# GpSimd's ring of gathers written out for six turns, and eighteen waits behind its drain

## The chip, the cores and the metric

The kernel runs on one core of one Trainium2 chip. The metric is the device time of one execution in microseconds. A profile is one recorded execution; its span runs from the first to the last instruction of the program and is shorter than the device time.

## What is computed

```python
def reference(x, lengths, w):            # x: 8 x 8192 x 512 float32, w: 512 x 512
    mask = (pos < lengths[:, None, None])
    cs = np.cumsum(x * mask, axis=1)
    midpoints = (lengths // 2).clip(0)
    mid_features = cs[b_idx, midpoints, :]
    return np.matmul(mid_features[:, None, :], w).squeeze(1)
```

For each of the 8 sequences, the rows of x from the first to the one at half the sequence's length are added up, and the sum is multiplied by w. The lengths are data, so the program learns only when it runs how many rows it has to read.

## The kernel before, in words

**The sum as a matrix product.** Rows of x lie on 128 partitions, and TensorE multiplies them by a small matrix of zeros and ones with one column for each sequence. A row that doesn't belong to a sequence's first half gets a zero. The products are accumulated in the PSUM tiles `s_ps` and `d_ps`.

**Three sources of rows.** The first 256 rows of every sequence are read whatever the lengths are. Rows 64 to 255 are loaded by two transfers on SyncE's queue at the start, into two slots of the tile `xt`. Rows 0 to 63 go into `xb`, by two transfers that GpSimd issues at the end (line 257). All rows from 256 on are gathered in units of 8 rows, 128 units (2 MiB) at a time, by an indirect DMA that GpSimd issues (line 228, in `fetch`). With the given lengths there are 13 gathers. They go round the three slots of `xt` (`R = 3`).

**The engines' parts in the round.** TensorE waits for a slot's data, multiplies it (line 395) and counts `s_done` up. ScalarE waits for that count, copies the next column of unit numbers into `now` (line 185, `s_now`) and the next zeros and ones into `ww`. GpSimd waits for `s_now`, issues the gather into the slot that has come free, and takes `s_now` back (line 252). SyncE relays the landings to TensorE. Each engine's round is a ring of program blocks: the function `ring` writes out `R` turns; before each the engine compares a register with the turn's number (line 126) and leaves the ring when no turn is left; after the last one it lowers the register (line 130) and jumps back (line 131). The first three gathers stand ahead of GpSimd's ring (blocks `gp_b_0` to `gp_b_2`).

**The end.** Behind its ring GpSimd issues six transfers: two for `xb`, and four for w into `wt`: a half (line 259), a quarter (line 261) and the two halves of the last quarter (line 263; `s_w[3]` counts the last of them). Then it runs a drain (line 264), and waits for the two stores of the output (`s_out` at 32, line 265, carried by the branch of line 266). TensorE waits for `xb` (`s_back`), for the copies of the sums into SBUF by VectorE and ScalarE, and for each piece of w, and multiplies the sums by w into `o_ps`. VectorE and ScalarE copy that to `o_sb`; SyncE and ScalarE store one half each (line 207). The branch leads GpSimd to the program's end, where all engines meet and GpSimd clears the semaphores.

Of the kernel before, what the change touches and what calls it, by code (L numbers as in the profile page):

```python
# [15 lines left out]
def kernel(  # L16
# [22 lines left out]
    R = 3  # L39
# [6 lines left out]
    C = -(-B * (S // 2 // U + 1 - HU) // P)  # L46
    FAR = 1 << 17
    IDLE = 2
    xu = x.rearrange("b (q u) d -> (b q) (u d)", u=U)
    lens_words = lengths.tensor.reshape([B]).bitcast(I32).ap().rearrange("(o t) -> o t", o=1)  # L50

# [8 lines left out]
    def sem(name):  # L60
        return tc.alloc_semaphore(name)
# [45 lines left out]
    s_back = [sem(f"back{k}") for k in range(PARTS)]  # L107
    s_w = [sem(f"w{k}") for k in range(4)]
# [11 lines left out]
    def weights_by_rows(at, n):  # L120
        return ww[:, at * B:(at + n) * B].rearrange("p (u b) -> p u b", b=B)

    def ring(eng, name, left, body):
        for s in range(R):
            with nc.body(f"{name}_0_{s}", valid_engines=[eng.engine]):
                eng.br_cmp(left, s, f"{name}_1_{s}", f"{name}_end", "IS_GT")  # L126
            with nc.body(f"{name}_1_{s}", valid_engines=[eng.engine]):
                body(s)
                if s == R - 1:
                    eng.reg_sub(left, left, R)  # L130
                eng.br(f"{name}_0_{(s + 1) % R}")


    def sync(sp):
        left = sp.alloc_register("left_sp")
        full = sp.alloc_register("full_sp")
        have = sp.alloc_register("have_sp")
        sp.reg_mov(full, 16)
        sp.reg_mov(have, 1)
        sp.wait_ge(s_dve, marks["count"])  # L140
        sp.load(left, count[:])
        sp.wait_ge(s_dve, marks["front"])
        sp.wait_ge(s_zero, 3)
        for f in range(PARTS):
            sp.wait_ge(s_front[f], 16)
            sp.sem_inc(s_rdy, 1)
        sp.br("sy_0_0")

        def relay(s):
            sp.wait_ge(s_wr, have)  # L150
            sp.wait_ge(s_full[s], full)
            sp.sem_inc(s_rdy, 1)
            sp.reg_add(have, have, 1)
            if s == R - 1:
                sp.reg_add(full, full, 16)

        ring(sp, "sy", left, relay)
        with nc.body("sy_end", valid_engines=[sp.engine]):
            sp.wait_ge(s_dve, marks["out0"])
            sp.wait_ge(s_act, 3)  # L160
            store(sp, 0)
            sp.br(END)


    def scalar(act):
# [16 lines left out]
        def weigh(s):  # L182
# [7 lines left out]
            act.reg_add(turn, turn, 1)  # L190

        ring(act, "ac", left, weigh)
        with nc.body("ac_end", valid_engines=[act.engine]):
            act.wait_ge(s_pe, 2)
# [15 lines left out]
    def gpsimd(pool):  # L210
        pool.iota(v_i[:], pattern=[[P * U, C], [1, U]], base=HEAD, channel_multiplier=0)
        pool.iota(r_i[:, FU:], pattern=[[2, BU], [-(BU // 2), FB]], base=0,
                  channel_multiplier=BU // 2).then_inc(s_pool, 1)
        pool.wait_ge(s_pool, 1)
        for k in range(4):
            pool.iota(at_i[32 * k:32 * k + 32], pattern=[[P, C]],
                      base=64 * (k % 2) + 8 * (k // 2) + 63 * 8 * k,
                      channel_multiplier=16).then_inc(s_pool, 1)
        pool.tensor_scalar(out=row[:, 2 * B + 2:], in0=lens[:, ::2], scalar1=0.5, scalar2=0.25,
                           op0=ALU.mult, op1=ALU.add)._wait_ge(s_len, 16).then_inc(s_pool, 1)  # L220
        pool.wait_ge(s_pool, 6)
        pool.iota(r_i[:, :FU], pattern=[[2, FU], [-(FU // 2), FB]], base=2 * TOP,
                  channel_multiplier=FU // 2)
        pool.iota(fold_i[:], pattern=[[-32, 2], [-1, B]], base=P, channel_multiplier=1,
                  ).then_inc(s_pool, 1)

        def fetch(to, units, at, n, full):
            return pool.indirect_dma_start(  # L228
                out=to, out_offset=None, in_=units,
                in_offset=bass.IndirectOffsetOnAxis(ap=at, axis=0),  # L230
                bounds_check=n - 1, oob_is_err=False).then_inc(full, 16)

        left = pool.alloc_register("left_pool")
        pool.wait_ge(s_dve, marks["idx"])
        pool.br("gp_b_0")
        for c in range(R):
            if c > 0:
                with nc.body(f"gp_a_{c}", valid_engines=[pool.engine]):
                    pool.br_cmp(left, c, f"gp_b_{c}", "gp_end", "IS_GT")
            with nc.body(f"gp_b_{c}", valid_engines=[pool.engine]):  # L240
                got = fetch(xt[:, c], xu, now[:, c:c + 1], B * UB, s_full[c])
                if c > 0:
                    got._wait_ge(s_done, c)
                if c == 0:
                    pool.load(left, count[:])  # L245
                if c == R - 1:
                    pool.reg_sub(left, left, R)
                pool.br(f"gp_a_{c + 1}" if c + 1 < R else "gp_0_0")

        def gather(s):  # L250
            fetch(xt[:, s], xu, now[:, s:s + 1], B * UB, s_full[s])._wait_ge(s_now, 1)
            pool.sem_inc(s_now, -1)  # L252

        ring(pool, "gp", left, gather)
        with nc.body("gp_end", valid_engines=[pool.engine]):
            for f in range(PARTS):
                pool.dma_start(out=xb[:, f], in_=x[FB * f:FB * (f + 1), :TOP].rearrange(  # L257
                    "b (q u) d -> q b (u d)", u=BU)).then_inc(s_back[f], 16)
            pool.dma_start(out=wt[:, :2], in_=w[HALVES[0]].rearrange("(p k) d -> p k d", k=2),
                           ).then_inc(s_w[0], 16)  # L260
            pool.dma_start(out=wt[:, 2], in_=w[QUARTERS[2]]).then_inc(s_w[1], 16)
            for g, at in enumerate(HALVES):
                pool.dma_start(out=wt[:, 3, at], in_=w[QUARTERS[3], at]).then_inc(s_w[2 + g], 16)  # L263
            pool.drain()
            pool.wait_ge(s_out, 32)
            pool.br(END)

# [125 lines left out]
    def tensor(pe):  # L393
# [5 lines left out]
        def idle(n):  # L399
            for _ in range(n):  # L400
                pe.matmul(idle_ps[:FB], lhsT=ones[:, :FB], rhs=ones[:, :1].to_broadcast((P, D)),  # L401
                          start=True, stop=True, skip_group_check=True)
# [24 lines left out]
        with nc.body("pe_idle", valid_engines=[pe.engine]):  # L427
            idle(IDLE)
            pe.br("pe_to")
# [4 lines left out]
        with nc.body("pe_end", valid_engines=[pe.engine]):  # L434
# [17 lines left out]
            for k in range(KC):  # L452
# [10 lines left out]

    programs = [(nc.vector, vector, "dv"), (nc.sync, sync, "sy"), (nc.scalar, scalar, "ac"),
                (nc.gpsimd, gpsimd, "gp")]
    for f in range(PARTS):
        nc.sync.dma_start(out=xt[:, f + 1, :FU * D], in_=x[FB * f:FB * (f + 1), TOP:HEAD].rearrange(
            "b (q u) d -> q b (u d)", u=FU)).then_inc(s_front[f], 16)
    nc.scalar.dma_start(out=lens[:], in_=lens_words).then_inc(s_len, 16)
    left = nc.tensor.alloc_register("left_pe")  # L470
# [37 lines left out]
```

## Time and profile before

| what | value |
|---|---|
| device time, median of 3 (lowest, highest) | 83.02 us (82.86, 83.16) |
| span of the profiled execution | 80.4 us |
| busy: TensorE, VectorE, ScalarE, GpSimd | 59.6, 11.8, 9.7, 19.9 us |
| bytes read from HBM over the span | 32.51 MB |
| a gather's issue on GpSimd, from issue to landing | 0.98 us, 11.7 us |
| start of one gather to the start of the next in the ring | 4.9 us |

In a group's row the page gives line, engine, operation, tiles and shape, the number of instructions, then the busy time, the mean of one in nanoseconds, and the idle time ahead of them with what ended it. Engine names: PE is TensorE, PEld its weight loads, DVE is VectorE, ACT ScalarE, POOL GpSimd, SP SyncE; a small q behind a name (POOLq) marks what the engine's sequencer does alone, such as branches, semaphore and register steps. They are not counted as busy. The busy TensorE is in part idle work: 58 of its multiplications write `idle_ps`, which nothing reads.

### The profile page before, as it was taken

What the parts mean: (1) busy time and instruction counts of PE and PEld (TensorE: products, weight loads), DVE (VectorE), ACT (ScalarE), POOL (GpSimd) and SP (SyncE); (2) the same over time, 40 slices, a digit from 0 to 9 for tenths busy, and PEclk for the clock granted to TensorE, in tenths of its full rate; (3) what the DMA queues carried; (4) which work ended last, traced back from release to release, by engine and by line L of the source; (5) the groups of instructions that cost most, each with busy time, mean ns of one, the idle gap of its engine ahead of it and who ended that gap; (6) DMA issues with size and microseconds to landing.
All of it is one profiled execution on the core that took longest, in us unless ns stands there. A gap on an engine that the chain in (4) does not pass through costs nothing.

```text
span 80.4 us, 1176 instructions
## 1 busy us (share of the span) xinstructions
PE 59.6 (74%) x360; PEld 14.1 (18%) x360; DVE 11.8 (15%) x43; ACT 9.7 (12%) x31; POOL 19.9 (25%) x32
## 2 busy tenths in 40 slices
PE   0599998997693957939488493975939679399940
PEld 0212212120110202112020110201102021112820
DVE  0799300891000000000000000000000000003130
ACT  2971010102010010201001020010100100000220
POOL 5432050754022040310404004040220793000000
PEclk9999999999999999999999999999999999999998
DMA  0899999999999999999999999999999999999700
GB/s 0 299 428 434 442 418 432 432 424 448 399 456 416 432 432 432 440 399 448 432 415 448 432 424 416 432 448 399 448 432 424 416 432 448 399 373 409 285 0 8
DMA packets 2803, 31.23 MB, mean 388 GB/s; under 512 B 434, under 2 KB 450, under 8 KB 962
## 3 DMA queue, kind: packets, MB, share of 16 engines
q0 software_dynamic: 2480, 28.05, 82.4%
q1 hardware_dynamic: 304, 3.15, 9.7%
q8 instruction: 1, 0.02, 0.1%
q10 hardware_dynamic: 18, 0.01, 0.0%
HBM read 32.51 MB, written 0.02 MB: 404 GB/s over the span
## 4 chain that ended last, share of the span: by engine, by line
issue 59%; POOL 14%; DMA 14%; PE 5%; DVE 2%; POOLq 2%; ACTq 0%; SPq 0%
POOL xt L228 14%; DMA xb<-in_x_dram 12%; DMA lens<-in_lengths_dram 1%; PE mf_ps L446 1%; PE o_ps L395 1%; PE d_ps L395 1%; PE bc_ps L408 1%; DVE o_sb L276 1%; POOL xb L257 1%; POOLq L245 1%; PE mf_ps L449 1%; POOLq L228 0%; DVE row L276 0%; POOLq L126 0%; DVE ge L276 0%
## 5 line engine op out<-in xcount | busy, mean ns | idle before, releaser
L395 PE MATMUL s_ps<-xt,ww 128*8 128x512 f32 x240 | 29.5, 598 | 14.6 <-PEq L415 14.6
L401 PE MATMUL idle_ps<-ones 128*4 128x512 f32 x58 | 29.6, 637 | 0.0
L228 POOL DMA_INDIRECT xt<-in_x_dram,now x13 | 14.8, 1135 | 45.9 <-POOLq L252 36.7
L395 PEld LDWEIGHTS s_ps<-xt,ww 128*8 128x8 f32 x240 | 5.9, 89 | 37.8 <-issue 37.6
L276 DVE COPY s_sb<-s_ps 128x256 f32<-128x256 f32 x2 | 0.8, 420 | 55.3 <-PE s_ps L395 55.3
L401 PEld LDWEIGHTS idle_ps<-ones 128*4 128x4 f32 x58 | 5.1, 90 | 20.4 <-issue 20.4
L185 ACT COPY now<-idx 128x1 int32 x10 | 1.9, 192 | 44.1 <-PE s_ps L395 44.1
L276 DVE TENSOR_TENSOR early<-v_f,ends 128x192 f32<-128x192 f32 (+1 forms) x2 | 2.4, 1192 | 5.5 <-PE s_ps L395 5.5
L408 PE MATMUL bc_ps<-row,ones 1*128 1x26 f32 x2 | 0.6, 396 | 2.9 <-DVE p L276 2.9
L188 ACT COPY ww<-wc 128x64 f32 x10 | 2.4, 244 | 0.1
L276 DVE TENSOR_TENSOR wc<-early,ge 128x192 f32<-128x192 f32 (+1 forms) x2 | 2.4, 1192 | 0.1
L166 ACT ACTIVATE xt<-xt 128x2048 uint32<-128x2048 uint32 x1 | 1.9, 1910 | 0.0
L196 ACT COPY d_sb<-d_ps 128x128 f32<-128x128 f32 x2 | 0.4, 268 | 12.1 <-PE d_ps L395 12.1
L178 ACT COPY ww<-wc 128x64 f32<-128x64 f32 x3 | 0.7, 244 | 8.2 <-PE s_ps L395 6.8
L166 ACT ACT_TABLE_LOAD x1 | 1.3, 1283 | 1.5 <-SPq L52 1.5
L395 PE MATMUL d_ps<-xb,ww 128*8 128x256 f32 x16 | 1.3, 388 | 0.1
L446 PE MATMUL mf_ps<-fold,s_sb 128*128 128x8 f32 x8 | 1.3, 265 | 0.0
L257 POOL DMA_DIRECT2D xb<-in_x_dram x2 | 1.2, 614 | 0.0
L446 PEld LDWEIGHTS mf_ps<-fold,s_sb 128*128 128x128 f32 x8 | 1.1, 197 | 0.4 <-DVE s_sb L276 0.4
L263 POOL DMA_DIRECT2D wt<-in_w_dram x2 | 1.2, 647 | 0.0
L395 PE MATMUL o_ps<-wt,mf_sb 128*8 128x128 f32 x32 | 1.1, 273 | 0.0
L408 PEld LDWEIGHTS bc_ps<-row,ones 1*128 1x128 f32 x2 | 0.5, 308 | 2.9 <-DVE p L276 2.9
(47 smaller groups left out, 14.1 us busy)
## 6 DMA issues: line engine op xcount, KB each, us to landing
xt<-in_x_dram SPq DMA_DIRECT2D x2, 1536.0 KB, 8.3
xb<-in_x_dram POOLq DMA_DIRECT2D x2, 512.0 KB, 9.4
wt<-in_w_dram POOLq DMA_DIRECT2D x1, 512.0 KB, 10.5
wt<-in_w_dram POOLq DMA_DIRECT2D x1, 256.0 KB, 10.7
wt<-in_w_dram POOLq DMA_DIRECT2D x2, 128.0 KB, 10.4
xt<-in_x_dram,now POOLq DMA_INDIRECT x13, 11.7
lens<-in_lengths_dram ACTq DMA_DIRECT2D x1, 0.1 KB
out_dram<-o_sb SPq DMA_DIRECT2D x1, 8.0 KB
```

The source lines that it names most:

```text
L166: act.memzero(xt[:, 1:, FU * D:]).then_inc(s_zero, 1)
L185: act.copy(out=now[:, s:s + 1], in_=idx[:, bass.ds(c, 1)]).then_inc(s_now, 1)
L188: act.copy(out=weights_of(s), in_=wc[:, bass.ds(c, 1)].rearrange("p c e -> p (c e)"),).then_inc(s_wr, 1)
L228: return pool.indirect_dma_start(out=to, out_offset=None, in_=units, in_offset=bass.IndirectOffsetOnAxis(ap=at, axis=0), bounds_check=n - ...
L245: pool.load(left, count[:])
L257: pool.dma_start(out=xb[:, f], in_=x[FB * f:FB * (f + 1), :TOP].rearrange("b (q u) d -> q b (u d)", u=BU)).then_inc(s_back[f], 16)
L263: pool.dma_start(out=wt[:, 3, at], in_=w[QUARTERS[3], at]).then_inc(s_w[2 + g], 16)
L276: do(*args, **kw).then_inc(s_dve, 1)
L395: return pe.matmul(to[32 * j:32 * j + weights.shape[1], :rows.shape[1]], lhsT=weights, rhs=rows, start=start, stop=False, skip_group_check ...
L401: pe.matmul(idle_ps[:FB], lhsT=ones[:, :FB], rhs=ones[:, :1].to_broadcast((P, D)), start=True, stop=True, skip_group_check=True)
L408: pe.matmul(bc_ps[:, :3 * B + 2], lhsT=ones[:1], rhs=row[:], start=True, stop=True,)._wait_ge(s_dve, marks["row"]).then_inc(s_pe, 1)
L446: pe.matmul(mf_ps[i][:, B * (k % 2):B * (k % 2 + 1)], lhsT=s_sb[:, QUARTERS[k]], rhs=fold[:], start=(k % 2 == 0), stop=False, skip_group_c ...
```

## The change

`ring` takes a number of turns. GpSimd's ring gets six in place of three, two rounds over the three slots, so the register is lowered and the jump back taken after six gathers; the other rings stay at three. Behind the drain GpSimd now waits for each of its six last transfers, and then twelve times (`PAD`) for w's last piece, before it waits for the output's stores. The further turns and the waits lengthen GpSimd's code, and the waits keep it busy, or waiting, between the drain and the end. All that is computed and transferred stays.

```diff
+    PAD = 12
...
-    def ring(eng, name, left, body):
-        for s in range(R):
+    def ring(eng, name, left, body, turns=R):
+        for s in range(turns):
             with nc.body(f"{name}_0_{s}", valid_engines=[eng.engine]):
                 eng.br_cmp(left, s, f"{name}_1_{s}", f"{name}_end", "IS_GT")
             with nc.body(f"{name}_1_{s}", valid_engines=[eng.engine]):
-                body(s)
-                if s == R - 1:
-                    eng.reg_sub(left, left, R)
-                eng.br(f"{name}_0_{(s + 1) % R}")
+                body(s % R)
+                if s == turns - 1:
+                    eng.reg_sub(left, left, turns)
+                eng.br(f"{name}_0_{(s + 1) % turns}")
...
-        ring(pool, "gp", left, gather)
+        ring(pool, "gp", left, gather, 2 * R)
...
             pool.drain()
+            for landed in (*s_back, *s_w):
+                pool.wait_ge(landed, 16)
+            for _ in range(PAD):
+                pool.wait_ge(s_w[3], 16)
             pool.wait_ge(s_out, 32)
             pool.br(END)
```

## The prediction

> **What bounds the kernel now.** I read the page from the top first, to see which resource is never idle, then the chain that ended last, then the stretches of its end, and at last the instructions of GpSimd's sequencer line by line, because the change touches nothing else.
>
> From the page:
>
> ```profile
> span 80.4 us, 1176 instructions
> DMA  0899999999999999999999999999999999999700
> GB/s 0 299 428 434 442 418 432 432 424 448 399 456 416 432 432 432 440 399 448 432 415 448 432 424 416 432 448 399 448 432 424 416 432 448 399 373 409 285 0 8
> q0 software_dynamic: 2480, 28.05, 82.4%
> q8 instruction: 1, 0.02, 0.1%
> ```
>
> Each digit is a slice of 2.0 us. The transfers are at 9 tenths or more from slice 3 to slice 37, at about 430 GB/s, and no engine's row is like that. 31.2 MB at 430 GB/s are 72.6 us: the stream is the span up to its end. The reader should also keep the last line in mind: one packet of instructions is fetched inside the span.
>
> The chain that ended last, from where the stream ends (start, length, what):
>
> ```profile
> 57.74 0.04 POOLq L130
> ...
> 58.05 4.50 issue
> 62.55 0.02 POOLq L252
> 62.57 0.06 issue
> 62.64 0.05 POOLq L126
> 62.69 0.10 issue
> 62.78 0.99 POOL xt L228
> 63.77 0.56 POOL xb L257
> 64.33 9.75 DMA xb<-in_x_dram
> 74.09 0.04 issue
> 74.13 0.64 PE d_ps L395 x8
> ```
>
> The pieces called "issue" of some 4.5 us before each gather are GpSimd waiting for the next index. When it issues xb at 64.33 the transfer still takes 9.75 us, since two to three gathers are queued ahead of it. So GpSimd's issuing runs about ten microseconds ahead of the data, and a tenth of a microsecond on it in the ring is hidden twice over.
>
> The end, by stretches (us, PE busy, ..., DMA share, GB/s), and the two instructions of GpSimd that stand around the change:
>
> ```profile
> 64.00:74.10 10.10, 7.85 (x60) 1.71 (x60) 0.44 (x2) 0.00 (x0) 3.10 (x6) 1.00 0.99 409
> 74.10:77.30 3.20, 3.12 (x52) 2.35 (x52) 0.68 (x4) 0.45 (x3) 0.00 (x0) 1.00 0.59 220
> 77.30:80.40 3.10, 0.00 (x0) 0.00 (x0) 0.55 (x2) 0.50 (x2) 0.00 (x0) 0.92 0.02 5
> ```
> ```profile
> L264 POOLq DRAIN  x1: 11993/11993/11993, 65.6 to 65.6; - x1
> ```
> ```profile
> L266 POOLq COMPARE_BRANCH  x1: 43/43/43, 79.3 to 79.3; - x1
> ```
>
> After the data come 3.2 us of TensorE, two copies that end at 77.88, and the stores, issued at 77.64 and 77.98. GpSimd's drain lasts from 65.56 to 77.55. Then GpSimd waits for both stores in the wait on its last branch, which starts at 79.32. From there GpSimd leads the closing exchange of all engines to 80.40. The median time, 83.02, is 2.6 us more than the span.
>
> **What the Trainium skill says.** "Perfetto Trace Analysis", section "DMA Instruction — SWDGE (GPSIMD)", says that such an instruction's recorded end is the end of writing descriptors, not of the transfer. The trace agrees: L257, L259, L261 and L263 take 0.61 to 0.65 us each, and land 9 to 11 us after issue. "Sequencer-only Instruction (DRAIN, etc)" on the same page says that a record starts when its semaphores are satisfied. So an added wait that is already satisfied shows as a short record, and costs the step to the next one. "Runtime: NRT & Kernel Launch", section "Instruction fetch mechanics", says that each engine's instructions come in 16 KiB blocks by a DMA of its own, and that a taken branch to a block that isn't held stalls for the fetch. The trace has one such packet of 16 KiB (0.02 MB above), in the answer for the stretch from 75 us; it starts at 76.05 and takes 1.10 us. It doesn't say which engine's it is. "DMA: Bandwidth & Descriptors", section "Queues, rings and completion order", says that a DMA engine turns between queues at packet boundaries only, so a small fetch can stand behind data for a while; no row here shows how long.
>
> **The change part by part.**
> *The ring of six turns.* Ten gathers run in the ring (13 less the three ahead of it). Before, the register is lowered and the ring jumps back after each third: at 28.39, 43.05 and 57.74. After, this happens once. From the record of L252 to that of L126 a plain turn takes 23.40 to 23.48, 0.08 us, and one with the jump back 28.30 to 28.60, 0.30 us. Two jumps less save 2 x 0.22 = 0.44 us of GpSimd's sequencer, in front of waits of 4.5 us each for the index. On the path: 0. What it does add is code: three more turns of about five instructions, some 15.
>
> *The six waits for xb and w.* The last of them lands 10.3 us after its issue at 66.45, so at about 76.7; the drain ends at 77.55. All six are satisfied when they are reached. *The twelve waits on w's last piece* are satisfied too. Together 18 sequencer steps. Semaphore steps in the chain take 0.08 us from one start to the next (18.52 to 18.60, 62.55 to 62.64); a register step takes 0.06 to 0.07. I take 0.08: 18 x 0.08 = 1.44 us, so GpSimd reaches its wait for the stores at 77.55 + 1.44 = 78.99. It is released at 79.32 in any case, so 0.33 us is left. Bounds: at 0.065 us it is there at 78.7. At the 0.18 us that the step from L266 (79.32) to the next record (79.50) takes, with its jump, it would be there at 80.8. Straight code has no jump, so the upper bound is unlikely. What is queued behind these waits is the wait for the stores, the branch, and the closing exchange, for which all engines wait; no transfer and no computation stands behind them.
>
> *Nothing is moved*: the same 13 gathers, the same six transfers at the end, the same drain. Sum on the path: 0 + 0 = 0, with the stores' landing hiding the waits, and 33 more instructions in GpSimd's code. At 64 bytes each (16 KiB for 256, by the page on the runtime) these are an estimated 2.1 KB, so whatever follows the drain, the closing exchange included, lies 2.1 KB further on.
>
> That leaves the place of the code as the only thing by which the time can move much. The profile cannot show where the blocks of GpSimd's code end, so here I cost both ways.
>
> **The rivals.**
> *No change (0.28).* As above: 83.0.
>
> *Faster by cheaper closing steps (0.26).* From the stores' landing to the end of the span there are 1.1 us led by GpSimd, and 2.6 us of the time lie outside the span. The first jump alone has a gap of 79.36 to 79.50, 0.13 us, where a straight step has 0.03 to 0.06. If the new place saves that 0.1, and a tenth of the 2.6 us at the program's ends, it is 0.1 + 0.26, so 82.7. For it: this piece is on the path with nothing beside it. Against it: no record shows GpSimd late there by more than that gap.
>
> *Faster by a fetch taken out of the end (0.12).* The drain ends 0.83 us after w's last landing, and 0.40 us after the fetched packet, 77.15. If the fetch is GpSimd's, the 33 instructions move it. In the profiled execution it starts when w is all but over. In others it may come ahead of xb's last packets, on which the chain stands at 74.09. One of 16 engines at 430 GB/s moves 16 KiB in 0.61 us, and the packet took 1.10: 0.6 to 1.1 us less on the path, 82.2. Against it: the three times lie within 0.3 us, so it would have to hit all of them, and TensorE too was near the end of its long code at that moment, so the fetch may be its own.
>
> *Slower by a fetch behind the drain (0.20).* If the boundary of a block now falls among the added waits, and the next block isn't held, GpSimd stands still from about 78.0 to 78.5 for at least the 1.1 us of the packet and 0.4 us to land, and up to about twice that. It comes to the stores' wait at 79.5 to 81.5 in place of 78.99, so 0.2 to 2.2 us late; in the middle 1.0: 84.0. For it: there is no slack beyond 0.33 us. Against it: a block fetched ahead of need costs nothing.
>
> *Slower by the waits themselves (0.07).* At 0.12 us a step, 18 take 2.16 us, to 79.7, 0.4 us late: 83.4.
>
> *Slower by a fetch in the ring or at its end (0.07).* The gathers' code grows ahead of the issue of xb. A stall behind the full queues, up to one gather (4.9 us), would drain the stream; with two gathers in flight some 3 us of it would show: 86.
>
> **How the numbers follow.** The likeliest single case is no change, 83.0. The faster cases have 0.26 + 0.12 = 0.38 together, the slower ones 0.20 + 0.07 + 0.07 = 0.34. That no step of the sum is on the path is well supported; that the place of the code doesn't matter is not, and the changes of place could cost or gain more than 0.25 us (0.3%). The range from 82.3 to 84.4 leaves out the ones with a gain beyond 0.7 us (half of 0.12), the stall in the ring (0.07) and the longer half of the fetch behind the drain (some 0.06): 0.19 in all.
>
> **What would show it.** Right: GpSimd's gathers start 4.9 us apart as before; the drain ends at about 77.5; 18 short records follow at 0.08 us each and end before 79.1; L266's successor starts within 0.05 us of the stores' landing at 79.3; the closing exchange takes 1.1 us. A fetch stall would be a gap of over 1 us among the 18 records, with an instruction packet in it, and a branch start after the stores' landing. A changed place of the fetch would be an instruction packet at another time than 76.05, or one more of them. Waits that are too dear would be steps over 0.097 us (1.74 us from 77.55 to 79.29 over 18). If the gain is in the part outside the span, the span stays 80.4 and the time falls. The prediction is wrong if the span moves with no change in these places.

## The result and the profile after

The changed kernel is slower: 83.67 us median (83.54 to 84.02) against 82.92 (82.86 to 83.16) for the kernel before, six runs of each. The ratio is 1.0089 with a 95% interval of 1.0067 to 1.0112.

From the page of the changed kernel:

```profile
span 81.5 us, 1181 instructions
DMA  0899999999999999999999999999999999999200
GB/s 0 319 422 422 430 432 410 442 442 402 450 426 410 458 426 402 458 426 402 458 434 394 458 434 394 458 434 394 458 434 394 450 442 394 394 410 400 99 12 0
q8 instruction: 1, 0.02, 0.1%
q14 instruction: 1, 0.01, 0.0%
```

The stream is the same, and so is the packet on q8. New is the last line: one more packet of instructions inside the span, half as large, on another queue.

The chain that ended last, in the changed kernel:

```profile
64.47 9.77 DMA xb<-in_x_dram
74.24 0.04 issue
74.28 0.64 PE d_ps L400 x8
...
77.75 0.29 DVE o_sb L281
```

xb lands at 74.24 in place of 74.09, and the last copy ends at 78.04 in place of 77.88. The 3.8 us of computation between are untouched. The 0.15 us ahead of it are no part of the explanation: over all profiles below xb lands between 73.97 and 74.61, and these two extremes come from one and the same kernel. What has grown is the stretch behind the chain. By stretches (us, PE busy and count, weight loads, VectorE, ScalarE, GpSimd, clock, DMA share, GB/s):

```profile
74.25:77.46 3.21, 3.12 (x52) 2.35 (x52) 0.66 (x4) 0.46 (x3) 0.00 (x0) 1.00 0.57 209
77.46:81.54 4.08, 0.00 (x0) 0.00 (x0) 0.55 (x2) 0.49 (x2) 0.00 (x0) 0.60 0.02 6
```

The last stretch was 3.10 us before and is 4.08 now, with no engine busy but in the same four copies.

GpSimd's new waits in two parts of that stretch (77.70 to 78.10, then 78.10 to 78.80), by the view of one line's instructions (count, durations in ns, first and last start):

```profile
L269 POOLq EVENT_SEMAPHORE  x4: 42/43/43, 77.7 to 78.0; - x4
```
```profile
L269 POOLq EVENT_SEMAPHORE  x4: 43/43/43, 78.5 to 78.7; - x4
```
```profile
L270 POOLq EVENT_SEMAPHORE  x1: 43/43/43, 80.3 to 80.3; - x1
```

One instruction carries two waits, so there are eight steps ahead of the wait for the stores, not eighteen, 0.087 us apart. They start right behind the drain, and between the fourth and the fifth (78.01 and 78.48) lie 0.47 us in place of 0.087: a pause of 0.38 us. Still, GpSimd stands at L270 by 78.83. It is released only at 80.33, where before its branch started at 79.32. So the waits were done in time, and the stores themselves came late.

The stores' transfers, between 79.10 and 79.60 (40 slices of 12.5 ns; a packet's bytes stand in the slice in which it starts):

```profile
GB/s 0 0 0 655 0 0 0 0 0 0 0 0 0 0 0 0 0 0 0 0 0 0 0 0 0 0 0 0 0 82 0 0 0 0 0 0 0 0 0 0
q14 instruction: 1, 0.01, 4.0%
q10 hardware_dynamic: 3, 0.00, 0.8%
```

The large packet is the 8 KB of instructions. It starts at 79.15 and takes 0.32 us. Seven of the eight packets of ScalarE's store had started by 79.02, and the eighth starts at 79.47, when the instructions are over. The landings of the two stores count up to 79.50, and the last one, for that packet, comes at 80.31. Before, the last two came at 79.27 and 79.29.

Part by part, from the two profiled executions:

| part | before | after | difference |
|---|---|---|---|
| xb's landing | 74.09 | 74.24 | +0.15 |
| from there to the last store's landing | 5.21 | 6.06 | +0.86 |
| from there to the end of the span | 1.15 | 1.24 | +0.09 |
| time outside the span | 2.47 | 2.15 | -0.33 |
| time of this execution | 82.92 | 83.69 | +0.77 |

Each figure is rounded by itself, from the nanoseconds of the traces.

The +0.09 is one more step of 0.087 on the path: the wait for the stores is carried by L270, ahead of the branch, and no longer by the branch itself. The last row but one is a gain that the span doesn't show at all. In the kernel before, the trace has a packet behind the end of the span, at 80.4; here between 82.50 and 83.00 (slices of 12.5 ns):

```profile
GB/s 0 0 0 0 0 0 0 0 0 0 0 0 0 0 0 0 0 0 655 0 0 0 0 0 0 0 0 0 0 0 0 0 0 0 0 0 0 0 0 0
q14 instruction: 1, 0.01, 5.5%
```

These are 8 KB on the same queue, at 82.73. The changed kernel has no packet behind its span.

### The profile page after: what moved, and what is told of

Its sections match the earlier page's. It is cut to its first block, busy times and chain, and to the rows that moved or that the text cites. A ratio compares the mean times of both kernels' runs of the same rounds, so it can differ in the third digit from the quotient of the medians.

```text
span 81.5 us, 1181 instructions
## 1 busy us (share of the span) xinstructions
PE 58.8 (72%) x360; PEld 14.0 (17%) x360; DVE 11.8 (15%) x43; ACT 9.7 (12%) x31; POOL 19.9 (24%) x32
## 4 chain that ended last, share of the span: by engine, by line
issue 56%; POOL 16%; DMA 13%; PE 5%; DVE 2%; POOLq 2%; ACTq 0%; SPq 0%
POOL xt L229 16%; DMA xb<-in_x_dram 12%; DMA lens<-in_lengths_dram 1%; PE mf_ps L451 1%; PE o_ps L400 1%; PE d_ps L400 1%; PE bc_ps L413 1%; DVE o_sb L281 1%; POOL xb L258 1%; POOLq L246 1%; PE mf_ps L454 1%; POOLq L229 0%; POOLq L127 0%; DVE row L281 0%; DVE z L281 0%
## 5 line engine op out<-in xcount | busy, mean ns | idle before, releaser
L400 PE MATMUL s_ps<-xt,ww 128*8 128x512 f32 x240 | 28.7, 592 | 15.6 <-PEq L420 15.5
L406 PE MATMUL idle_ps<-ones 128*4 128x512 f32 x58 | 28.8, 621 | 0.0
```

Source lines behind the costliest of these rows:

```text
L400: return pe.matmul(to[32 * j:32 * j + weights.shape[1], :rows.shape[1]], lhsT=weights, rhs=rows, start=start, stop=False, skip_group_check ...
```

## The theories and the experiments

**Fetch theory.** GpSimd's code comes in blocks. Passing from one to the next pauses its sequencer for 0.38 us and sets off a transfer of 8 KB of instructions about 1.1 us after the last step ahead of the pause. In the changed kernel both come at the end, and the transfer holds up a packet of the second store. **Waits theory**: the eighteen waits on GpSimd are the cost. **Ring theory**: the ring of six moves the stream. The edits below are against the changed kernel, unless it is said otherwise.

### The ring alone

```diff
-            for landed in (*s_back, *s_w):
-                pool.wait_ge(landed, 16)
-            for _ in range(PAD):
-                pool.wait_ge(s_w[3], 16)
```

> The ring of six turns alone; the eighteen waits behind the drain are left out. GpSimd's code up to the drain is as long as in the changed kernel; the point at which the changed kernel's sequencer paused (between the 4th and the 5th step behind the drain) now lies in the closing exchange, after the stores have landed. Fetch theory (crossing a block of code pauses GpSimd's sequencer for about 0.4 us and starts an 8 KB instruction transfer about 1.1 us later, which costs more only where it meets the stores): last store lands at about 79.4 as before, a pause of about 0.4 us between two closing steps, span about 80.9, time 83.2 to 83.4. Waits theory (the waits are the cost): 82.9. Ring theory (the ring of six moves the stream): 83.6.

Measured: ratio 1.0003 (0.9983 to 1.0022), 83.17 us. The stores land at 79.44. The pause is where it was expected, in the closing exchange: two steps of GpSimd that were 0.08 us apart start at 79.82 and 80.28. The instructions come at 80.97, far behind the stores. The exchange takes 1.57 us in place of 1.15, yet the time is that of before: the 0.32 outside the span are gone here too (2.15), and 0.42 - 0.32 = 0.10 us is the difference of the medians (83.17 and 83.07). So the fetch theory had the place and the stores right, and its time was up to 0.2 too high (83.2 to 83.4), because it didn't yet count that gain. The ring theory falls: the same ring, and the stores are in time.

### The waits alone

```diff
-        ring(pool, "gp", left, gather, 2 * R)
+        ring(pool, "gp", left, gather)
```

> The eighteen waits alone, with GpSimd's ring of three turns. Fetch theory: the code is 15 instructions shorter ahead of the drain, so no pause among the waits and no instruction transfer at 79 us; the waits take 9 x 0.087 = 0.8 us from 77.6 and end by 78.5; last store lands at 79.3 to 79.4; time 82.8 to 83.0. Waits theory: 83.6 as in the changed kernel. Ring theory: 82.9.

Measured: ratio 1.0028 (1.0012 to 1.0044), 83.31 us. None of the theories had this. The eight steps of L269 run through without a pause (77.97 to 78.58), the last store lands at 79.70, 0.04 us behind the one before it, and GpSimd goes on at once. So the waits are not what costs 0.7 us. The pause comes later, in the closing exchange, behind the clearing of the semaphores (80.46, then 81.06; 0.22 us apart before), and the exchange takes 1.76 us in place of 1.15. There it is on the path, as in the run above. The +0.61 is made up of the pause of 0.38, the step of 0.087, and 0.13 for a drain behind the pause that takes 0.16 us in place of 0.03. Less 0.42 outside the span (2.05) this is +0.19, against 0.24 in the medians (83.31 and 83.07). The 8 KB packet comes at 81.75, behind the end of the span.

### The same code, the padding's waits a little later

```diff
             for _ in range(PAD):
-                pool.wait_ge(s_w[3], 16)
+                pool.wait_ge(s_dve, marks["out1"])
```

> The changed kernel with the same code length, but the twelve waits of the padding wait for VectorE's last copy (about 78.0) in place of w's last piece, so all of them and the pause fall about 0.35 us later. Fetch theory: pause from about 78.4 to 78.8, instruction transfer at about 79.5, after the stores' packets (78.6 to 79.1); last store lands at 79.4 to 79.5 and the waits are done by 79.2; time 82.9 to 83.1. Waits theory and ring theory: 83.6, as the waits are no fewer and end later.

Measured: ratio 0.9964 (0.9945 to 0.9982), 82.76 us. This is the run that tells most: the same number of instructions and of waits, and the loss is gone. The transfers between 79.40 and 79.80, and the instruction that takes the stores' landing:

```profile
GB/s 0 0 0 0 0 0 819 0 0 0 0 0 0 0 0 0 0 0 0 0 0 0 0 0 0 0 0 0 0 0 0 0 0 0 0 0 0 0 0 0
q14 instruction: 1, 0.01, 4.8%
```
```profile
L270 POOLq EVENT_SEMAPHORE  x1: 43/43/43, 79.2 to 79.2; - x1
```

The instructions come at 79.46, with no packet of the stores in the stretch; those had all started by 78.78. The last two landings are 79.16 and 79.19. The pause is still there (78.07 to 78.54, between the same two steps), and costs nothing, since GpSimd would only have waited. That the time lies below that of before wasn't expected.

### The pause ahead of the drain

```diff
+            for _ in range(20):
+                pool.wait_ge(s_len, 16)
             pool.drain()
-            for landed in (*s_back, *s_w):
-                pool.wait_ge(landed, 16)
-            for _ in range(PAD):
-                pool.wait_ge(s_w[3], 16)
```

> Ring of six turns, no waits behind the drain, but twenty waits (ten instructions, on the lengths' transfer, long landed) between the last transfer's issue and the drain, so that the point of the pause lies ahead of the drain, at about 66 us. Fetch theory: an instruction transfer at 66 to 72 us in the stream, none near the stores; 8 KB more among 31 MB; last store at 79.3 to 79.4, time 82.8 to 83.0. Waits theory: 82.9, as these waits are hidden by the drain. Ring theory: 83.6.

Measured: ratio 0.9984 (0.9967 to 1.0002), 82.96 us. The pause is at 66.13 to 66.60, hidden by the drain, and the instructions come at 70.07, in the middle of the stream. That is 3.5 us behind the pause and not 0.7, as it is when no data are queued. The stores land at 79.64, the last 0.06 us behind the one before it. Without a pause on the path and with 2.15 us outside the span this kernel should have shown the gain of the one before it, and it showed 0.2 us less. The transfer took 0.31 us while all DMA engines were full, which is of that size; that it is the reason is not shown.

### The changed kernel again, and the pause earlier

The first of these is the kernel of the change, with no edit.

> The changed kernel itself, to have it beside the others on one chip. Fetch theory: instruction transfer at about 79.15 us, last store about 0.9 us after the one before it, 0.6 to 0.9 us slower than before in the times, and the profiled execution alike. If the late store was chance in one execution: no such gap between the last two landings, and times within 0.3 us of before.

Measured: ratio 1.0097 (1.0076 to 1.0119), 83.78 us. Instructions at 79.06 to 79.48, the last two landings at 79.37 and 80.22, and GpSimd's L270 at 80.24. It was no chance of one execution.

```diff
+            for _ in range(9):
+                pool.wait_ge(s_len, 16)
             pool.drain()
```

> The changed kernel with nine satisfied waits (on the lengths) ahead of the drain, four instructions, so that the pause falls on the first instruction behind the drain, some 0.4 us earlier than in the changed kernel. Fetch theory: instruction transfer at about 78.7 to 78.8 us and done at 79.1; it stands ahead of a packet of ScalarE's store (78.8 to 79.1) and the last landing is late by less than in the changed kernel if the transfer's end decides: at about 79.9, time 83.3 to 83.5; if it comes to lie between the two stores, 83.0. Waits theory: 83.7, as no wait is taken away.

Measured: ratio 1.0051 (1.0035 to 1.0066), 83.55 us. The instructions come at 78.92 to 79.49, and hold up a packet of each store: one of SyncE's and one of ScalarE's start at 79.49 and 79.54, when the others had started by 78.84 and 79.18. The last landings are 80.27 and 80.44. The time is 0.05 us above the range expected, and the last store was no less late than in the changed kernel, where 79.9 had been expected. The profiled execution (83.82) is the slowest of this kernel's four, so its landings are later than the usual ones.

### The ring of three with the code as long

```diff
-        ring(pool, "gp", left, gather, 2 * R)
+        ring(pool, "gp", left, gather)
...
+            for _ in range(31):
+                pool.wait_ge(s_len, 16)
             pool.drain()
```

> GpSimd's ring of three turns, with all eighteen waits, and 31 satisfied waits (15 instructions, on the lengths) ahead of the drain, in place of the three further turns: every instruction from the drain on has the place that it has in the changed kernel. Fetch theory: pause between the 4th and 5th step behind the drain, instruction transfer at about 79.15, last store late by 0.9 us, time 83.6 to 83.8. Ring theory: 83.0, as the ring is that of before.

Measured: ratio 1.0075 (1.0057 to 1.0092), 83.64 us: the loss is back, with the ring of before. I had the place wrong by three instructions: the pause lies between the first and the second step behind the drain (77.61 and 78.07), so a turn of the ring counts for one instruction less than I had taken, four and not five, as the records of a plain turn have it. The transfers between 78.70 and 79.20:

```profile
GB/s 0 0 0 82 164 655 82 0 0 82 0 0 0 164 0 0 1 0 0 0 0 0 0 0 0 0 0 0 0 0 0 0 0 0 0 82 0 0 0 0
q14 instruction: 1, 0.01, 4.8%
```

Here the instructions (slice 6, at 78.77) come in the midst of ScalarE's packets. Seven of those start from 78.75 to 78.86, and the eighth at 79.14, when the instructions end (79.15). It lands at 79.92, and the others by 79.33.

In all four profiles with the loss (the changed kernel, its repeat, the earlier pause and this one) the first store packet that is held up starts 3 to 4 ns before the instruction packet is over (79.469 and 79.473, 79.473 and 79.477, 79.491 and 79.494, 79.144 and 79.148). So the store's packet stood behind the instructions on the same DMA engine; the traces don't name the engine, but four coincidences of a few nanoseconds leave little room for another reading.

### Whether the gain is real, and a version made for it

The first and the last run here are the kernel with the later padding, with no further edit.

> The kernel in which the padding waits for VectorE's last copy, again, in five rounds. Fetch theory: the instruction transfer at 79.4 to 79.5 comes after the stores' packets, so the time is that of before: 82.9 to 83.1; the 0.3 us that this kernel had been below before is then chance. If something in it is a gain (the ring, or the place), it is 82.7 to 82.8 again and below before by 0.2 to 0.4 %.

Measured: ratio 0.9966 (0.9953 to 0.9979), 82.82 us against 83.08. The kernel with the later padding beats the kernel before and the changed one. In all profiles of kernels in which the pause comes inside the span, the part of the time outside it is 2.05 to 2.15 us; only in the kernel before it is 2.47. The single runs, with spans to 0.1 us, agree: in all 147 runs of the changed kernel and of the experiments it is 2.01 to 2.20 us. In the 126 runs of the kernel before that were made beside the experiments it is 2.33 to 2.64 in 111, and 2.07 to 2.20 in 15. So in the kernel before the pause, 0.38 us where it can be seen, comes behind the span and on the path, in most of its runs. The pause itself has no record there, but the 8 KB packet at 82.73 has.

The place in the code says the same. With the ring of three (the waits alone, the ring of three with the code as long, and the next run) the pause stands behind the 17th instruction that GpSimd's sequencer passes after the issue of the last of the six transfers. In the kernel before only 11 are recorded there, so the place lies beyond its last record. With the ring of six it stands behind the 5th, in all eight profiles, and three turns of four instructions are the difference.

```diff
+            for _ in range(33):
+                pool.wait_ge(s_len, 16)
+            pool.wait_ge(s_w[0], 16)
             pool.drain()
```

The diff is against the kernel before, with nothing added but waits ahead of its drain, so that the pause falls between w's first piece and the stores.

> The kernel before, with its ring of three and no wait behind the drain; ahead of the drain 33 satisfied waits (on the lengths) and one for w's first piece (75.4 us), so that the pause falls on the drain at about 75.5. Fetch theory: instruction transfer at about 76.5, when w's packets are over and the stores' have not begun; no pause later, so the part of the time outside the span is 2.15 us in place of the 2.47 of before, the last store lands at 79.3 as before, and the time is 0.3 us below before: 82.7 to 82.8. If the gain of the late padding comes from the ring of six or from GpSimd's being busy up to the end, this kernel is at 83.0 to 83.1 as before.

Measured: ratio 0.9970 (0.9954 to 0.9986), 82.73 us against 83.00. The drain, and the transfers between 76.50 and 77.10:

```profile
L267 POOLq DRAIN  x1: 1738/1738/1738, 76.0 to 76.0; - x1
```
```profile
q14 instruction: 1, 0.01, 4.2%
```

The wait for w's first piece starts at 75.50 and the drain 0.47 us later, which is the pause. The instructions come at 76.64 to 77.03, and no packet follows behind the span. The stores land at 79.38 and 79.43, and 2.14 us lie outside the span. The gain needs neither the ring of six nor a busy GpSimd.

> The kernel in which the padding waits for VectorE's last copy once more, beside the former: 82.7 to 82.9; one step of 0.087 us between the stores' landing and the branch that the former does not have, so the former is at most 0.1 us below it.

Measured: ratio 0.9984 (0.9966 to 1.0001), 82.84 us, beside the one above: 0.11 us between the two, of which the one step more is 0.09. Here the interval just touches no change; the three medians of this kernel are 82.76, 82.82 and 82.84, against 83.07, 83.08 and 83.00 for the kernel before.

## Why the prediction was wrong

**What held.** The stream and the gathers are as they were, and the two jumps saved show nowhere. The drain ends where it did. The waits are hidden by the stores' landing: GpSimd reached its wait at 78.83, and I had taken 78.99. I had that from the wrong sum (18 steps at 0.08; it is eight at 0.087 and a pause of 0.38), but the term is of the same size. The 33 more instructions are 21 in the records: four to a turn, and two waits to an instruction.

**The step that failed** is "The six waits for xb and w" with its conclusion, "no transfer and no computation stands behind them", and the sum "0 + 0 = 0, with the stores' landing hiding the waits". I took the stores' landing as fixed. Between waits that run out before it and a landing that doesn't move, nothing could cost anything. But GpSimd's passing through its code sets off a transfer itself, and that took 0.32 us on an engine on which a store's packet was due: the last landing came 0.80 and 0.85 us behind the one before it in place of 0.02 to 0.06 (in the changed kernel and its repeat).

**The rivals.** The nearest, "slower by a fetch behind the drain", had the place (a boundary of a block among the added waits) and the direction, and the wrong means: it let GpSimd stand still until the block had come, 1.5 us or more. GpSimd paused 0.38 us, went on, and was in time; it was the store that waited. The sum came out at 84.0 in place of 83.67 by luck. It was also given only 0.20. "Faster by cheaper closing steps" named a gain outside the span and guessed 0.26 us; there are 0.33 in the profile of the changed kernel and 0.32 to 0.42 in the others. The size was near by luck: no closing step got cheaper, but a pause of 0.38 us moved away from behind the span. The collision took the gain back more than twice over. "Faster by a fetch taken out of the end" rested on the 16 KiB packet at 76.05 being GpSimd's. It is there at 75.96 to 76.26 in eleven of the twelve profiles, wherever GpSimd's own pause lay, and at 77.15 in one. So it isn't GpSimd's.

**The evidence I had.** The page of before showed one instruction packet, and the code's length was known; where the next block begins couldn't be read from it. But the page ends with the span, and the trace goes on: the 8 KB packet at 82.73 could have been read there, and it is a sign that a fetch was due at about the program's end. It doesn't say which engine's, but longer code on GpSimd could bring it forward, towards the stores. Both outcomes that I gave for the place of the code (it doesn't matter, or it stalls) also left out that a fetch is traffic on the same engines as the stores. "DMA: Bandwidth & Descriptors" of the Trainium skill, section "Queues, rings and completion order", has what fits: a completion's increment lands only after every earlier write of that DMA engine, across its queues. The last landings here come 0.74 to 0.84 us after the end of the instruction packet in the changed kernel, its repeat and the ring of three, while a store's packet undisturbed lands about 0.35 to 0.4 us after its end. That the 0.4 more is this order is argued from the page and not shown apart from the rest by a run. "Runtime: NRT & Kernel Launch", section "Instruction fetch mechanics", gives blocks of 16 KiB and calls the cost of passing into the next one mostly hidden; here the packet that moved with GpSimd's code had 8 KB, and each pass paused the sequencer by 0.38 us, and hid only where GpSimd had nothing to do.

**What stays open.** Why 0.2 us are missing from the gain when the instructions come in the midst of the stream (the pause ahead of the drain) wasn't tried apart. The kernel before lacks the 0.3 to 0.4 us outside the span in 15 of 126 runs; why is not known, since no profile of such a run was kept.

## What to carry to other kernels

An instruction that waits for nothing still moves all code behind it, and the passing into the next block of code is an event with a time: look for instruction packets in the list of queues, see which transfers stand beside them, and place the event where the engine waits anyway and no short transfer on the path is due. A gain or loss of some tenths of a microsecond from waits that are all satisfied can be a hint of that, and the check is to keep the instructions and to move them in time only. Compare the time outside the span as well as the span, since a kernel's end can hide a pause there, and ask the trace for the packets behind the span.

## What was not expected of the hardware

- GpSimd's sequencer pauses 0.38 us at one point of its code (seen in eleven of the twelve profiles; in nine of them a step of 0.46 to 0.47 us in place of 0.08 to 0.09), at another step when the code ahead of it has another length, and an instruction transfer of 8 KB follows: 1.1 to 1.4 us after the last step ahead of the pause when few data are queued, 3.9 us after it in the full stream.
- A packet of 1 KB held up for 0.3 to 0.5 us by 8 KB of instructions completes 0.6 to 0.9 us late (79.33 to 79.92, 79.50 to 80.31, 79.37 to 80.22).
- GpSimd's drain ends 0.83 to 0.86 us behind the last landing of GpSimd's transfers (76.72 and 77.55 before, 76.87 and 77.70 after), and in the version made for the gain, where it is issued at 75.96, just as well (76.84 and 77.70).
- Two waits share one sequencer instruction, which takes 0.087 us from start to start.
